# Attention with its sums of squares in the outputs' PSUM bank, later rotation ends, moved ramp buffers and fewer small softmax operations

## Chip, cores, metric

The kernel runs on one core of a Trainium2 chip. The core has five engines, each with a queue of its own that it works off in order: TensorE (PE, matrix products; its weight loads are listed as PEld), VectorE (DVE), ScalarE (ACT), GpSimd (POOL) and SyncE (SP, which here only issues DMAs; POOL issues some as well). The metric is device time in microseconds; a kernel's time is the median of its runs.

## The reference, cut to what matters

Two layers over 528 tokens (16 learned meta tokens and 512 others) of width 2048. Layer 0 mixes tokens by softmax attention, layer 1 by gated linear attention. Around each: `h <- h + post_norm(mixer(pre_norm(h)))`. The change is mostly in layer 0:

```
def attention_mixer(h, w_in, q_norm, k_norm, w_out, ang_row, ang_col):
    q, k, v, gate = split(h @ w_in)          # 16 q heads, 8 k and v heads, of 128; gate of 2048
    q = apply_axial_rope(rmsnorm(q, q_norm), ang_row, ang_col)      # norm per head, then rotation
    k = apply_axial_rope(rmsnorm(k, k_norm), ang_row, ang_col)
    s = einsum(q, k) * 128 ** -0.5           # each k, v head serves two q heads
    p = softmax(s)
    o = einsum(p, v)
    return (o * silu(gate)) @ w_out
```

Layer 1 projects q, k, v, an output gate and two low-rank decay gates (one per direction), sums the log gates along the tokens, and computes decayed scores and outputs per head (4 heads). Its output, normed and gated, goes through `w_out`, is normed, added to `h`, and the 512 real tokens are stored.

## The kernel before, in words

**Precision.** Products of float32 are made of three products: each operand is split into a rounded part and a remainder (`split`: a cast on ScalarE, line 135, and a subtraction on VectorE, line 136), and high x high, high x low and low x high are summed in PSUM (lines 158 to 160 for the projections). So each weight block of 512 KB costs a DMA (`wraw`), a cast (`whi`) and a subtraction (`wlo`), and 48 matmuls for each half of the tokens (264 columns).

**Order of the work.** Instructions are written in the order of a clock kept in Python (`Clock`): each three projection matmuls of 264 columns step it by 0.339 us, so a projection of 128 columns of weights over both halves steps it by 10.84. Side work hangs on it: generators that `yield` a delay (`drive`), and functions put off by `after`. That gives a program order; the compiler's planner then places each instruction on its engine's queue by that priority, by when its buffers and inputs are free in its model, and it adds the semaphore waits. On the chip, the order of each queue is fixed.

**Stages.** (1) *Start*: `x` is loaded, transposed, and the first three gate columns projected. (2) *Ramp of layer 0*: K0, Q0, Q1, V0 are projected and stored in DRAM (`qkv_d`), then gates 3 to 12 by a seven-product scheme (`seven`; its combined inputs are `th`, `tl`, in the profile `t0h`, `t0l`; `quarters` are raw weight blocks, `y` the results on their way to `g_d`). (3) *Attention*: eight groups `g` of one k, v head and two q heads. While the scores and outputs of group g are computed (`attention`), the projections of group g + 1 are written between them (`qkv`: K, Q, Q, V; for g + 1 = 1 V comes first). Group 0 has no projection there; its tiles come back from DRAM (`first_group`, `one_head`). (4) *Output projection and residual*, the low-rank gates, a ramp of layer 1 that is like the first. (5) *Gated linear attention*, four heads. (6) *Last projection*, four token tiles in turn, each finished and stored by `finish_token`.

**What the change touches in stage 3.** `take` makes `qw` (the head times its norm weight) and `sq` (its squares) while evacuating the projection's PSUM banks (tag `pp`, three of them), lines 291 and 292. `rope` swaps the quarters of `qw` by four DMAs into `qs` (SP), splits `sq` into `sh`, `sl`, multiplies by cosine and sine on POOL (lines 304, 305), and puts off its end, `late`, by 3.7 of the clock: per half of the tokens two matmuls with ones (`ssq`, lines 310 and 311) that sum the squares over partitions, an evacuation on VectorE into `f`, which is the `sq` tile (line 312), then a reciprocal root on ScalarE, the two halves of the rotation added (line 314), times `f` (line 315), and split into `qh`, `ql` or `kh`, `kl`. `softmax` computes a block of scores `s` (128 queries x 528 keys, one pair of banks), its maximum (627), the maximum times -SCALE (628), the exponential with its sum (631), the reciprocal (632), and the scaling of `pn`: 512 columns (633), and the last 16 three times over, for an 80-row transposed operand (635). `transposed` transposes `pn` into `pT` and `pTm` (lines 641, 643; both with tag `t`, two banks in turn) and splits them into `ph`, `pl`, `pmt`. `weighted` accumulates the outputs in the one bank with tag `o` (lines 661 to 664), copied out by ScalarE (665). `values` transposes V by way of the `t` banks too (`vps`, `vpm`, lines 551 to 563). `stored_gates` loads gates, applies SiLU (line 610 on POOL) and stores gated outputs. Of PSUM's eight banks three are `pp`, two `s`, two `t`, one `o`. A block of scores takes one slot of the clock (`SLOTS[g]`), and there are nine blocks and a last step for each group.

**In stages 4 and 5.** `token_major` copies rows of `h` through `hb` to DRAM. `gates(h)` loads the low-rank weights of head h, splits them into `ups`, and makes log gates: `z` (matmul `pz`, line 1044; ScalarE, line 1045), `e`, and running sums. `load_v` brings V back through `vt`, one tile of 512 columns at a time, and splits it.

Of the kernel before, what the change touches and what calls it, by code (L numbers as in the profile page):

```python
# [10 lines left out]
F32 = mybir.dt.float32  # L11
# [8 lines left out]
P = 128  # L20
D = 2048
# [13 lines left out]
AHEAD = 400  # L35
SLOTS = (2.6, 3.8, 3.8, 3.8, 3.8, 3.8, 3.8, 2.6)

# [45 lines left out]
def hybrid_encoder(  # L83
# [201 lines left out]
    def take(wcol):  # L285

        qw = wk.tile([P, T], F32, tag="qw", name="qw")
        sq = wk.tile([P, T], F32, tag="sq", name="sq", bufs=1)

        def evac(ps, a, b):  # L290
            A.activation(qw[:, a:b], ps, AF.Copy, scale=wcol)
            A.activation(sq[:, a:b], ps, AF.Square)
        return qw, sq, evac

    def rope(qw, sq, outs, ps_t):
        qs = wk.tile([P, T], F32, tag="qs", name="qs", bufs=1)
# [10 lines left out]
        def late():  # L307
            for a, b in HALVES:
                ps = ps_t.tile([P, 512], F32, tag="t", name="ssq")[:, :b - a]
                PE.matmul(ps, ones_r, sh[:, a:b], start=True, stop=False)  # L310
                PE.matmul(ps, ones_r, sl[:, a:b], start=False, stop=True)
                V.scalar_tensor_tensor(f[:, a:b], ps, 1.0 / P, erow[:, a:b], op0=ALU.mult, op1=ALU.add)
            rsqrt_inplace(f)
            V.tensor_tensor(qw, qw, qs, op=ALU.add)
            V.tensor_tensor(qw, qw, f, op=ALU.mult)
            for hi, lo, a, b in outs:
                split(hi, lo, qw[:, a:b])
        clk.after(3.7, late)

# [168 lines left out]

    la = ExitStack()
    yp = pool(la, "yp0", 2)  # L490
    ta = pool(la, "ta0")
    quarters = [ta.tile([P, 4 * HALF], F32, name=f"x0{i}") for i in range(4)]
    th, tl = [ta.tile([P, KH, 4 * HALF], F32R, name=f"t0{w}") for w in "hl"]

# [34 lines left out]
    REP = 80  # L529
    pn_bufs = [pb.tile([P, T + REP], F32, name=f"pn{i}") for i in range(NP)]  # L530
    for t in pn_bufs:
# [6 lines left out]
    def values(g):  # L538
# [4 lines left out]
        if g == 0:  # L543
            nc.gpsimd.dma_start(out=vt, in_=qkv_d[3])
        else:
# [30 lines left out]
    def first_group(outs):  # L576

        qws = []
        for i in range(4):
            if i < 3:  # L580
                qws.append(wk.tile([P, T], F32, tag="qw", name="qw"))
                nc.gpsimd.dma_start(out=qws[i], in_=qkv_d[i])
            if i:
                one_head(qws[i - 1], outs[i - 1], i - 1)
            yield 3.8

    def one_head(qw, outs, i):
        sq = wk.tile([P, T], F32, tag="sq", name="sq", bufs=1)
        A.activation(sq, qw, AF.Square)
        A.activation(qw, qw, AF.Copy, scale=col(QN if i else KN))  # L590
        rope(qw, sq, outs, ps_t)

# [26 lines left out]
    def softmax(n, qh, ql, kh, kl):  # L619
# [6 lines left out]
        sm = wa.tile([P, 1], F32, tag="sm", name="sm")[:n]  # L626
        V.reduce_max(mx, s, axis=AX.XY)  # L627
        V.tensor_scalar(mx, mx, -SCALE, None, op0=ALU.mult)  # L628
        pn = pn_bufs[n_pn[0] % NP][:n]
        n_pn[0] += 1  # L630
        A.activation(pn[:, :T].rearrange("p (a b) -> p a b", a=2), s, AF.Exp, bias=mx, scale=SCALE, accum_out=sm)  # L631
        V.reciprocal(sm, sm)
        V.tensor_scalar(pn[:, :SEQ], pn[:, :SEQ], sm, None, op0=ALU.mult)
        for r in (0, 32, 64):
            V.tensor_scalar(pn[:, T + r:T + r + META], pn[:, SEQ:T], sm, None, op0=ALU.mult)
        return pn

    def transposed(pn, n, puts):
# [3 lines left out]
        pm = ps_t.tile([P, 512], F32, tag="t", name="pTm")[:REP]  # L642
        PE.transpose(pm[:, :n], pn[:, T:], ident[:n, :n])
        for (ph, pl, pmt), qc, c, m in puts:
# [59 lines left out]
    for g in range(KV):  # L704
        o_sb = o_tiles()
        att = attention(qk, vv, o_sb, SLOTS[g])
        att = clk.drive(att if g else chain(first_group(first_outs), att))
        gates = [] if g == 0 else [2 * g - 2, 2 * g - 1]
# [10 lines left out]
        if g + 1 < KV:  # L719
# [130 lines left out]
    def token_major(k, t):  # L850
# [7 lines left out]
        A.activation(hb, ps, AF.Square, accum_out=s1[:n, t, k // 4:k // 4 + 1])  # L858
# [98 lines left out]
    quarters += [ta.tile([P, 4 * HALF], F32, name=f"x{i}") for i in range(2, 4)]  # L957

    def token_rows(ys, vc):

        c = slice(vc * P, (vc + 2) * P)
        for ts in ((0, 1), (2, 3), (4,)):
# [6 lines left out]
            for n, t in enumerate(ts):  # L969
# [55 lines left out]


    def gates(h):
        ur = g2.tile([P, SEQ], F32, tag="gr", name="ur", bufs=1)[:16].rearrange("p (d n) -> p d n", d=2)
        nc.sync.dma_start(out=ur, in_=gla_gk_up[0, :, :, h * 256:(h + 1) * 256].rearrange("d r n -> r d n"))
        yield 4.0  # L1030
        A.copy(ups[0:16], ur)
        A.copy(ups[64:80], ur)
        V.tensor_tensor(ups[32:48], ur, ups[0:16].bitcast(F32), op=ALU.subtract)
# [327 lines left out]
    def finish_token(t, ps):  # L1361
# [3 lines left out]
        A.activation(r, r, AF.Exp, scale=-0.5)  # L1365
        for n in range(2):
            ns = slice(n * 1024, (n + 1) * 1024)
            V.scalar_tensor_tensor(y[t][:, ns], y[t][:, ns], r, h1[t][:, ns], op0=ALU.mult, op1=ALU.add)
# [52 lines left out]
```

## Time and profile before

| | |
|---|---|
| median of 3 runs | 1814.77 us (1813.13 to 1814.82) |
| the profiled execution | 1812.24 us, of which the span of the profile is 1810.5 us |
| mean granted clock of TensorE | 0.995 |

The profile is of one execution. Busy shares are of the span. A row of the stages has from and to, the length, the busy time and count of each engine, the granted TensorE clock (1.00 is full), the busy share of the DMA engines, and GB/s. A row of waits has the waiting engine with the tile that it writes and its line, what it waited for, and the sum, the number and the longest of the waits. A row of instructions has the start, the duration, engine, line, operation, output <- inputs, and in brackets the idle time before it with what ended it. A row of one line's instructions has the shortest, the median and the longest duration in ns, and when the first and the last started. A DMA row of the page has its count, the size of one and the median time from issue to landing.

### The profile page before, as it was taken

How to read it: one execution, taken by the hardware profiler on the slowest of the kernel's cores; microseconds unless marked ns; L12 is line 12 of the kernel's file. 1: busy time of each engine (PE TensorE's matmuls, PEld its weight loads, DVE VectorE, ACT ScalarE, POOL GpSimd, SP SyncE). 2: the span in 40 equal slices, each digit the busy share in tenths (PEclk: the TensorE clock that was granted, in tenths of full speed). 3: DMA queues.
4: the chain of work that ended last, by engine and by line, in shares of the span. 5: the costliest groups of instructions: out<-in, count | busy, mean ns of one | idle time of the engine just before them, and what ended most of it. 6: DMA issues, size and time to landing. Idle time of an engine off the chain costs nothing. (4 is left out here: it accounts for less than half of the span.)

```text
span 1810.5 us, 31970 instructions
## 1 busy us (share of the span) xinstructions
PE 1764.6 (97%) x12591; PEld 1656.8 (92%) x12591; DVE 1147.3 (63%) x2118; ACT 951.1 (53%) x1909; POOL 218.1 (12%) x291
## 2 busy tenths in 40 slices
PE   8999889999999999999999999999999999999998
PEld 7999888999999999999999999988898988888886
DVE  5777578766766766752229787758585765764224
ACT  5543456555555555553328544468575775853221
POOL 3100222112121111111111101110000100000000
PEclk9999989999999999999999999999999999999999
DMA  8444422323233233153336344343332332354323
GB/s 255 143 140 119 153 75 86 89 83 95 71 95 95 60 95 112 66 174 86 91 96 201 118 140 118 106 136 89 86 108 71 108 101 80 100 157 169 98 93 128
DMA packets 266453, 203.12 MB, mean 112 GB/s; under 512 B 9884, under 2 KB 239840, under 8 KB 265776
## 3 DMA queue, kind: packets, MB, share of 16 engines
q1 hardware_dynamic: 254480, 162.52, 31.3%
q0 software_dynamic: 11824, 38.57, 6.1%
q8 instruction: 99, 1.62, 0.4%
q14 instruction: 50, 0.41, 0.1%
HBM read 165.47 MB, written 29.09 MB: 107 GB/s over the span
## 5 line engine op out<-in xcount | busy, mean ns | idle before, releaser
L158 PE MATMUL pp<-uh,whi 128*128 128x264 f32 (+1 forms) x2320 | 711.8, 307 | 1.2 <-POOL whi L357 0.6
L159 PE MATMUL pp<-ul,whi 128*128 128x264 f32 (+1 forms) x2320 | 702.7, 303 | 2.3 <-DVE ul L419 2.3
L160 PE MATMUL pp<-uh,wlo 128*128 128x264 f32 (+1 forms) x2320 | 703.3, 303 | 0.3 <-POOL wlo L358 0.3
L136 DVE TENSOR_TENSOR wlo<-wraw,whi 128x1024 fp32r<-128x1024 f32 (+1 forms) x239 | 293.5, 1229 | 289.1 <-ACT whi L135 288.3
L160 PEld LDWEIGHTS pp<-uh,wlo 128*128 128x128 f32 x2320 | 437.5, 189 | 17.5 <-POOL wlo L358 0.6
L158 PEld LDWEIGHTS pp<-uh,whi 128*128 128x128 f32 x2320 | 437.6, 189 | 17.2 <-POOL whi L357 0.9
L159 PEld LDWEIGHTS pp<-ul,whi 128*128 128x128 f32 x2320 | 438.0, 189 | 16.2 <-DVE ul L419 2.7
L135 ACT CAST whi<-wraw 128x1024 fp32r<-128x1024 f32 (+1 forms) x239 | 249.1, 1043 | 291.5 <-PE pp L159 95.2
L135 ACT CAST whi<-x 128x1024 fp32r<-128x1024 f32 x48 | 50.1, 1047 | 71.4 <-PE pp L236 55.5
L631 ACT ACTIVATE pn<-s,mx 128x528 f32<-128x528 f32 (+1 forms) x72 | 50.4, 700 | 67.0 <-DVE mx L628 61.8
L1333 PE MATMUL f<-whi,ul 128*128 128x512 f32 x192 | 75.6, 394 | 0.0
L1331 PE MATMUL f<-whi,uh 128*128 128x512 f32 x192 | 75.5, 393 | 0.0
L1332 PE MATMUL f<-wlo,uh 128*128 128x512 f32 x192 | 75.3, 392 | 0.0
L237 PE MATMUL pp<-uh,wlo 128*128 128x264 f32 x264 | 75.2, 285 | 0.0
L235 PE MATMUL pp<-uh,whi 128*128 128x264 f32 x264 | 75.0, 284 | 0.0
L236 PE MATMUL pp<-ul,whi 128*128 128x264 f32 x264 | 74.7, 283 | 0.0
L136 DVE TENSOR_TENSOR wlo<-x,whi 128x1024 fp32r<-128x1024 f32 x48 | 58.6, 1222 | 20.0 <-ACT whi L135 19.9
L304 POOL TENSOR_TENSOR qw<-qw,cos 128x528 f32<-128x528 f32 x24 | 32.2, 1340 | 287.4 <-DMA qs<-qw 261.0
L646 DVE TENSOR_TENSOR pl<-pT,ph 128x512 fp32r<-128x512 f32 (+1 forms) x80 | 47.3, 592 | 17.1 <-ACT ph L645 16.7
L627 DVE TENSOR_REDUCE mx<-s 128x1 f32<-128x528 f32 (+1 forms) x72 | 50.7, 704 | 8.9 <-PE s L624 7.6
L645 ACT CAST ph<-pT 128x512 fp32r<-128x512 f32 (+1 forms) x80 | 40.4, 505 | 30.0 <-PE pT L641 24.2
L235 PE MATMUL pp<-th,whi 128*128 128x264 f32 x192 | 55.8, 292 | 0.0
(401 smaller groups left out, 3734.5 us busy)
## 6 DMA issues: line engine op xcount, KB each, us to landing
wraw<-in_attn_w_in_dram SPq DMA_DIRECT2D x82, 512.0 KB, 4.2
wraw<-in_gla_w_in_dram SPq DMA_DIRECT2D x81, 512.0 KB, 3.9
wraw<-in_attn_w_out_dram SPq DMA_DIRECT2D x32, 512.0 KB, 3.9
wraw<-in_gla_w_out_dram SPq DMA_DIRECT2D x32, 512.0 KB, 3.8
x<-in_gla_w_in_dram SPq DMA_DIRECT2D x15, 512.0 KB, 4.4
qs<-qw SPq DMA_DIRECT2D x96, 66.0 KB, 3.1
x<-in_attn_w_in_dram SPq DMA_DIRECT2D x12, 512.0 KB, 4.3
x<-h_d SPq DMA_DIRECT2D x32, 132.0 KB, 3.2
```

The source lines that it names most:

```text
L135: A.copy(hi, src)
L136: V.tensor_tensor(lo, src, hi.bitcast(F32), op=ALU.subtract)
L158: PE.matmul(ps, wh, uh[:, k, a:b], start=first, stop=False)
L159: PE.matmul(ps, wh, ul[:, k, a:b], start=False, stop=False)
L160: PE.matmul(ps, wl, uh[:, k, a:b], start=False, stop=last)
L235: PE.matmul(ps, w[0][:, k], bh[:, k], start=k == 0, stop=False)
L236: PE.matmul(ps, w[0][:, k], bl[:, k], start=False, stop=False)
L237: PE.matmul(ps, w[1][:, k], bh[:, k], start=False, stop=k == KH - 1)
L627: V.reduce_max(mx, s, axis=AX.XY)
L1331: PE.matmul(ps, uh[:, k, ts], wh[:, kk], start=(k == 0), stop=False)
L1332: PE.matmul(ps, uh[:, k, ts], wl[:, kk], start=False, stop=False)
L1333: PE.matmul(ps, ul[:, k, ts], wh[:, kk], start=False, stop=(k == KT - 1))
```

## The change

- `rope`: the `ssq` matmuls of both halves go to the outputs' bank (tag `o`) instead of the `t` banks; the end comes 6.5 of the clock later (4.5 for group 0's heads) instead of 3.7. `qw` has three buffers instead of two, `sq` two instead of one.
- The norm weight of q is multiplied by SCALE once; the maximum is negated by the reduction itself; the multiplication by -SCALE goes. The three copies of the last 16 columns become one operation with a broadcast input.
- Ramp of layer 0: `th`, `tl` are placed first in memory, `y` and the quarters behind them.
- Group 0: all three loads of `qw` are issued at the start; V's load goes to SP's queue; the heads follow at 1.0, 4.6, 4.6 and 5.0 instead of 3.8 each. Group 0's slot is 3.1 instead of 2.6; group 1's scores start 7.0 later.
- Layer 1: the low-rank weights of head 0 are loaded and split (`up_rows`) ahead of the ramp's projections; the forward `z` tiles of head 0 lie in `vt`'s buffer; `load_v(0)` has no delay of 16 any more; `hb` has four buffers instead of five.
- `finish_token`: the last token tile is finished in pieces of 1024, 640 and 384 columns instead of 1024 and 1024.

```diff
-SLOTS = (2.6, 3.8, 3.8, 3.8, 3.8, 3.8, 3.8, 2.6)
+SLOTS = (3.1, 3.8, 3.8, 3.8, 3.8, 3.8, 3.8, 2.6)
...
-        qw = wk.tile([P, T], F32, tag="qw", name="qw")
-        sq = wk.tile([P, T], F32, tag="sq", name="sq", bufs=1)
+        qw = wk.tile([P, T], F32, tag="qw", name="qw", bufs=3)
+        sq = wk.tile([P, T], F32, tag="sq", name="sq", bufs=2)
...
-    def rope(qw, sq, outs, ps_t):
+    def rope(qw, sq, outs, ps_t, wait=6.5):
...
-                ps = ps_t.tile([P, 512], F32, tag="t", name="ssq")[:, :b - a]
+                ps = ps_o.tile([P, 512], F32, tag="o", name="ssq")[:, :b - a]
...
-        clk.after(3.7, late)
+        clk.after(wait, late)
...
+    V.tensor_scalar(col(QN), col(QN), SCALE, None, op0=ALU.mult)
...
+    ta = pool(la, "ta0")
+    th, tl = [ta.tile([P, KH, 4 * HALF], F32R, name=f"t0{w}") for w in "hl"]
     yp = pool(la, "yp0", 2)
-    ta = pool(la, "ta0")
     quarters = [ta.tile([P, 4 * HALF], F32, name=f"x0{i}") for i in range(4)]
-    th, tl = [ta.tile([P, KH, 4 * HALF], F32R, name=f"t0{w}") for w in "hl"]
...
-            nc.gpsimd.dma_start(out=vt, in_=qkv_d[3])
+            nc.sync.dma_start(out=vt, in_=qkv_d[3])
...
-        for i in range(4):
-            if i < 3:
-                qws.append(wk.tile([P, T], F32, tag="qw", name="qw"))
-                nc.gpsimd.dma_start(out=qws[i], in_=qkv_d[i])
-            if i:
-                one_head(qws[i - 1], outs[i - 1], i - 1)
-            yield 3.8
+        for i in range(3):
+            qws.append(wk.tile([P, T], F32, tag="qw", name="qw", bufs=3))
+            nc.gpsimd.dma_start(out=qws[i], in_=qkv_d[i])
+        for i in range(3):
+            yield 4.6 if i else 1.0
+            one_head(qws[i], outs[i], i)
+        yield 5.0
...
-        V.reduce_max(mx, s, axis=AX.XY)
-        V.tensor_scalar(mx, mx, -SCALE, None, op0=ALU.mult)
+        V.reduce_max(mx, s, axis=AX.XY, negate=True)
...
-        for r in (0, 32, 64):
-            V.tensor_scalar(pn[:, T + r:T + r + META], pn[:, SEQ:T], sm, None, op0=ALU.mult)
+        V.tensor_scalar(pn[:, T:].rearrange("p (r m) -> p r m", r=3)[:, :, :META],
+                        pn[:, SEQ:T].unsqueeze(1).broadcast_to([n, 3, META]), sm, None, op0=ALU.mult)
...
-        att = clk.drive(att if g else chain(first_group(first_outs), att))
+        lead = first_group(first_outs) if g == 0 else iter([7.0] if g == 1 else [])
+        att = clk.drive(chain(lead, att))
...
+    ups = c1.tile([80, 2, 256], F32R, name="ups")
+    G.memset(ups.bitcast(F32), 0.0)
...
-        hb = t2.tile([P, 512], F32, tag="hb", name="hb", bufs=5)[:n]
+        hb = t2.tile([P, 512], F32, tag="hb", name="hb", bufs=4)[:n]
...
+    def up_rows(h, ur):
+        ur = ur.rearrange("p (d n) -> p d n", d=2)
+        nc.sync.dma_start(out=ur, in_=gla_gk_up[0, :, :, h * 256:(h + 1) * 256].rearrange("d r n -> r d n"))
+        yield 4.0
+        A.copy(ups[0:16], ur)
+        A.copy(ups[64:80], ur)
+        V.tensor_tensor(ups[32:48], ur, ups[0:16].bitcast(F32), op=ALU.subtract)
...
     built = clk.drive(combine(th, tl, quarters))
+    clk.drive(up_rows(0, sa.tile([16, SEQ], F32, name="ur", bufs=1)))
...
     def gates(h):
-        ur = g2.tile([P, SEQ], F32, tag="gr", name="ur", bufs=1)[:16].rearrange("p (d n) -> p d n", d=2)
...
+        if h:
+            yield from up_rows(h, g2.tile([P, SEQ], F32, tag="gr", name="ur", bufs=1)[:16])
...
-                z = g2.tile([P, T], F32, tag="z", name="z", bufs=1)[:, :n]
+                z = g2.tile([P, T], F32, tag="vt" if h == d == 0 else "z", name="z", bufs=1)[:, :n]
...
-        if h in (0, 3):
-            yield 24.0 if h else 16.0
+        if h == 3:
+            yield 24.0
...
-        for n in range(2):
-            ns = slice(n * 1024, (n + 1) * 1024)
+        for a, b in ((0, 1024), (1024, D)) if t < 3 else ((0, 1024), (1024, 1664), (1664, D)):
+            ns = slice(a, b)
```

More of the change, by code (lines that the diff above doesn't have):

```diff
@@ L529, in hybrid_encoder @@
     REP = 80
-    pn_bufs = [pb.tile([P, T + REP], F32, name=f"pn{i}") for i in range(NP)]
+    pn_bufs = [pb.tile([P, T + 96], F32, name=f"pn{i}") for i in range(NP)]
     for t in pn_bufs:
@@ L578, in first_group @@
         qws = []
-        for i in range(4):
-            if i < 3:
-                qws.append(wk.tile([P, T], F32, tag="qw", name="qw"))
-                nc.gpsimd.dma_start(out=qws[i], in_=qkv_d[i])
-            if i:
-                one_head(qws[i - 1], outs[i - 1], i - 1)
-            yield 3.8
+        for i in range(3):
[5 more added lines that the diff above has]
+        yield 5.0
     def one_head(qw, outs, i):
-        sq = wk.tile([P, T], F32, tag="sq", name="sq", bufs=1)
+        sq = wk.tile([P, T], F32, tag="sq", name="sq", bufs=2)
         A.activation(sq, qw, AF.Square)
         A.activation(qw, qw, AF.Copy, scale=col(QN if i else KN))
-        rope(qw, sq, outs, ps_t)
+        rope(qw, sq, outs, ps_t, 4.5)
     def stored_gates(hs, held):
@@ L626, in softmax @@
         sm = wa.tile([P, 1], F32, tag="sm", name="sm")[:n]
-        V.reduce_max(mx, s, axis=AX.XY)
-        V.tensor_scalar(mx, mx, -SCALE, None, op0=ALU.mult)
+        V.reduce_max(mx, s, axis=AX.XY, negate=True)
         pn = pn_bufs[n_pn[0] % NP][:n]
         n_pn[0] += 1
-        A.activation(pn[:, :T].rearrange("p (a b) -> p a b", a=2), s, AF.Exp, bias=mx, scale=SCALE, accum_out=sm)
+        A.activation(pn[:, :T].rearrange("p (a b) -> p a b", a=2), s, AF.Exp, bias=mx, accum_out=sm)
         V.reciprocal(sm, sm)
         V.tensor_scalar(pn[:, :SEQ], pn[:, :SEQ], sm, None, op0=ALU.mult)
-        for r in (0, 32, 64):
-            V.tensor_scalar(pn[:, T + r:T + r + META], pn[:, SEQ:T], sm, None, op0=ALU.mult)
+        V.tensor_scalar(pn[:, T:].rearrange("p (r m) -> p r m", r=3)[:, :, :META],
+                        pn[:, SEQ:T].unsqueeze(1).broadcast_to([n, 3, META]), sm, None, op0=ALU.mult)
         return pn
@@ L642, in transposed @@
         pm = ps_t.tile([P, 512], F32, tag="t", name="pTm")[:REP]
-        PE.transpose(pm[:, :n], pn[:, T:], ident[:n, :n])
+        PE.transpose(pm[:, :n], pn[:, T:T + REP], ident[:n, :n])
         for (ph, pl, pmt), qc, c, m in puts:
@@ L727, in hybrid_encoder @@
     slots = [wk.tile([P, T], F32, tag=tag, name="ogr", **kw) for tag, kw in
-             (("qw", {}), ("qw", {}), ("qs", dict(bufs=1)), ("sq", dict(bufs=1)))]
+             (("qw", dict(bufs=3)), ("qw", dict(bufs=3)), ("qs", dict(bufs=1)), ("sq", dict(bufs=2)))]
     slots.append(wa.tile([P, T], F32, tag="vt", name="ogr", bufs=1))
@@ L1005, in hybrid_encoder @@
     vm = cg.tile([80, 512], F32R, name="vm")
-    ups = cg.tile([80, 2, 256], F32R, name="ups")
     kfs = [cg.tile([P, 2, T], F32, name=f"kf{i}") for i in range(2)]
@@ L1011, in hybrid_encoder @@
     nc.sync.dma_start(out=qf[:, 0], in_=kq_d[2][:, :SEQ])
-    for t in am + [vm, ups]:
+    for t in am + [vm]:
         G.memset(t.bitcast(F32), 0.0)
@@ L1027, in gates @@
     def gates(h):
-        ur = g2.tile([P, SEQ], F32, tag="gr", name="ur", bufs=1)[:16].rearrange("p (d n) -> p d n", d=2)
[L1029 to L1033, printed above, removed]
+        if h:
+            yield from up_rows(h, g2.tile([P, SEQ], F32, tag="gr", name="ur", bufs=1)[:16])
         yield 2.0
```

## The prediction

> **What bounds the kernel now.** I read the busy times first, then the span cut into stages, then TensorE's waits.
>
> ```profile
> PE 1764.6 (97%) x12591; PEld 1656.8 (92%) x12591; DVE 1147.3 (63%) x2118; ACT 951.1 (53%) x1909; POOL 218.1 (12%) x291
> ```
>
> TensorE (PE) is busy 97% of the span, and the change alters the count or shape of no large matmul. What can be won is idle time of PE, and time at a lower clock. The stages (first column: from and to, in us; then length and busy time of each engine):
>
> ```profile
> 205.00:340.00 135.00, 120.36 (x926) 115.84 (x925) 95.53 (x218) 76.30 (x167) 31.75 (x34) 0.95 0.36 104
> 340.00:580.00 240.00, 230.76 (x1869) 225.66 (x1868) 168.35 (x401) 135.30 (x303) 45.82 (x43) 1.00 0.30 86
> 580.00:760.00 180.00, 177.88 (x1446) 174.22 (x1446) 130.03 (x330) 97.02 (x227) 22.76 (x21) 1.00 0.29 85
> 1180.00:1210.00 30.00, 27.36 (x176) 23.95 (x175) 13.53 (x19) 15.35 (x25) 6.83 (x15) 1.00 0.56 165
> 1210.00:1802.80 592.80, 592.22 (x3263) 511.37 (x3261) 353.75 (x620) 341.51 (x719) 23.40 (x43) 1.00 0.35 105
> 1802.80:1810.50 7.70, 0.00 (x0) 0.00 (x0) 3.23 (x4) 1.17 (x4) 0.00 (x0) 0.69 0.61 242
> ```
>
> Softmax attention (205 to 760) has 14.6 + 9.2 + 2.1 = 25.9 us of idle PE, the start of the gated layer 2.6, its remaining 593 us only 0.6, the tail 7.7. The waits of PE say who ends that idle time (total, times, longest):
>
> ```profile
> PE ssq L310 <- DVE pl L646: 8.6, 13, 1.3
> PE ssq L310 <- DVE vm L562: 6.8, 1, 6.8
> PE pT L641 <- DVE pn L633: 3.7, 2, 3.5
> PE s L622 <- ACT pn L631: 2.6, 2, 1.3
> PE pTm L643 <- DVE vl L555: 1.6, 3, 0.5
> PE pz L1044 <- ACT z L1045: 1.6, 1, 1.6
> PE s L622 <- ACT qh L135: 0.8, 1, 0.8
> PE pz L1044 <- DVE ups L1033: 0.7, 1, 0.7
> ```
>
> Two long stalls also cost clock. The stretches right behind them:
>
> ```profile
> 225.60:228.80 3.20, 3.15 (x14) 3.15 (x15) 2.44 (x4) 0.37 (x2) 1.75 (x2) 0.50 0.17 42
> 256.10:263.00 6.90, 6.49 (x27) 5.73 (x28) 5.21 (x11) 3.13 (x10) 3.05 (x2) 0.51 0.16 39
> ```
>
> The column before the last two is the granted clock. Behind the 6.8 us stall PE worked 3.15 us at half speed, which loses 1.6; behind the 3.5 us stall 6.49 us, which loses 3.2. The stalls of 1.3 us left no such stretch. So the ceiling is 25.9 + 2.6 + 1.6 + 3.2 = 33 us, 1.8%, unless the tail shrinks.
>
> In a sentence apart: the Trainium skill, TensorE: Matmul & The Clock Gate, Part 1, gives half clock after about 3.4 us idle and full clock after about 3.4 us of sustained work; by the latter the second stall would lose 1.7 instead of 3.2, and my sum would be 19.8 instead of 21.3. The trace shows 6.9 us, and the measurement decides.
>
> **The change part by part.**
>
> *Loads of group 0 (all three q/k tiles asked for at once, `vt` moved from POOL's queue to SP's, the ramp's `th`/`tl` placed where the attention's tiles come to lie, `y` and the quarters above).*
>
> ```profile
> 216.88 1.33 POOL L610 TENSOR_TENSOR gs<-gs,gr 128x528 f32<-128x528 f32 x1 [6.95 <-ACT gs L145]
> 218.18 1.11 POOL L582 DMA_DIRECT2D qw<-qkv_d  x2
> ACT sq L589 <- DMA qw<-qkv_d: 2.4, 1, 2.4
> 205.00:210.00 5.00, 5.00 (x43) 5.00 (x42) 2.09 (x3) 1.05 (x1) 2.60 (x7) 1.00 1.03 330
> L237 PE MATMUL pp<-t0h,wlo x160: 280/283/289, 109.4 to 202.5; 128*128 128x264 f32 x160
> ```
>
> The first head's loads leave POOL at 218.18, behind a multiplication that waited 6.95 us; ScalarE then stands 2.4 us on the landing, with the evacuations of `vps` queued behind it, `vm` comes last of these, and PE's `ssq` waits for the bank that `vm` reads: 6.8 + 1.6 = 8.4 us. In the new layout the tiles lie over `th`/`tl` (`t0h`, `t0l` in the profile), last read at 202.5 by the row above, not over the `y` tiles that are still being stored; the loads can leave some 10 us earlier, and `ssq` no longer shares a bank with `vps`. `vt` on SP is one issue among the weight loads, and one less on POOL. Late next is the rest of the head's chain, under 1.4 us of PE by my guess from the 1.3 us stalls above. I take 7.0 (bounds 0 and 8.4).
>
> *`sq` twice, `qw` three times, rotation's end at 6.5 instead of 3.7.*
>
> ```profile
> 247.23 0.84 ACT L291 ACTIVATE qw<-pp,cols 128x264 f32<-128x264 f32 x2
> 258.36 0.67 ACT L292 ACTIVATE sq<-pp 128x264 f32<-128x264 f32 x2
> DVE qw L314 <- POOL qs L305: 15.6, 13, 3.0
> ```
>
> Group 1's first head is copied out of PSUM at 247.23, but its squares only at 258.36, 11 us later: the single `sq` is still the factor of group 0's last head. So the projection banks stay full, PE has no projection to put between, and stands 3.5 us at `pT`. VectorE in turn stands 15.6 us in all at `L314` for POOL's rotation, with softmax work queued behind it; ending the rotation 2.8 later lets that work go first. With two `sq` the bank is freed at once. I take 6.0 of 3.5 + 3.2 (bounds 0 and 6.7), and 1.0 of the `s` waits of 2.6 + 0.8 (0 and 3.4). `ssq` later delays `kh`, `qh`; the 10.8 clock-us V projection of the code covers that, and group 1, whose V comes first, gets a lead of 7.0 before its scores.
>
> *Sums of squares in the outputs' bank.*
>
> ```profile
> 225.65 0.59 PE L310 MATMUL ssq<-sh,ones_r 128*128 128x264 f32 x1 [6.78 <-DVE vm L562]
> 229.23 0.28 PE L310 MATMUL ssq<-sh,ones_r 128*128 128x264 f32 x1
> L311 PE MATMUL ssq<-sl,ones_r x48: 280/284/422, 226.0 to 709.6; 128*128 128x264 f32 x48
> L312 DVE SCALAR_TENSOR_TENSOR sq<-ssq,erow x48: 419/423/435, 227.6 to 713.4; 128x264 f32<-128x264 f32 x48
> L315 DVE TENSOR_TENSOR qw<-qw,sq x24: 684/707/710, 232.5 to 715.3; 128x528 f32<-128x528 f32 x24
> ```
>
> `ssq` leaves the two banks of `pT`, so the 8.6 us on `pl` go. But the outputs have one bank: in each of the 24 rotations (48 halves) the second half's matmuls must wait until `L312` has read the first, at least 0.284 + 0.423 = 0.71 us, and an output that follows waits for the second read. The program order is laid out with other matmuls in such gaps: the halves at 225.65 and 229.23 lie 3.6 us apart with projections between. So the price is between 0 and 24 x 0.71 = 17.0. Nearest is what a half waited for so far, 8.6 / 48 = 0.18 each, since it is again VectorE running behind the order: 24 x 0.18 = 4.3. Net gain 4.3 (bounds 8.6 and -8.4).
>
> *Fewer small softmax operations.*
>
> ```profile
> L628 DVE TENSOR_SCALAR mx<-mx x72: 131/153/155, 249.4 to 754.6; 128x1 f32<-128x1 f32 x64, 32x1 f32<-32x1 f32 x8
> L635 DVE TENSOR_SCALAR pn<-pn,sm x216: 216/227/1349, 251.5 to 756.8; 128x16 f32<-128x16 f32 x96, 32x16 f32<-32x16 f32 x12
> ```
>
> 72 `L628` at 0.153 go: 11.0 us of VectorE. 216 `L635` become 72 of 48 elements; at 0.227 each (a little above, at most the 0.7 of the 528-element rows) some 33 us of VectorE go in all when summed by duration. The added scaling of one column is one operation like `L628`, beside PE's ramp. VectorE is not the bound (394 of 555 us busy in these stages), so PE gets only what waited on its tail: I take 1.0 (0 and the 1.6 of `pTm`).
>
> *Slots.* Group 0 takes 15.2 lead (as before: 4 x 3.8 = 1.0 + 4.6 + 4.6 + 5.0) plus ten slots: 41.2 clock-us before, 46.2 after; group 1 38 before, 45 after. Their cover is four projections, 43.4. The overrun of 2.8 + 1.6 = 4.4 is covered by the next group's projections, which need none of it: 0 (bounds 0 and a loss of 4.4).
>
> *Start of the gated layer.*
>
> ```profile
> L1031 ACT CAST ups<-ur x4: 602/619/620, 1194.9 to 1502.7; 16x512 fp32r<-16x512 f32 x4
> 1201.11 0.62 ACT L135 CAST vh<-vt 128x512 fp32r<-128x512 f32 x1 [0.74 <-DMA vt<-v_d]
> ```
>
> The first `ups` (one SP load, two casts of 0.62, a subtraction, a POOL memset) moves ahead of the ramp's projections, which cover it: the 0.7 goes. `z` takes `vt`'s buffer, so the V loads come behind the gates, and ScalarE no longer stands on a landing in the middle of their chain: most of the 1.6 goes. I take 2.0 (0 and 2.3). `load_v` without its delay of 16 starts later in effect, under projections.
>
> *`hb` 5 to 4.*
>
> ```profile
> h_d<-hb POOLq DMA_DIRECT2D x16, 256.0 KB, 3.6
> L858 ACT ACTIVATE hb<-ht x20: 571/588/623, 959.9 to 1008.8; 128x512 f32<-128x512 f32 x16, 16x512 f32<-16x512 f32 x4
> ```
>
> 20 in 49 us is one per 2.4; four buffers last 9.8, a store lands in 3.6: 0.
>
> *Last token tile in three pieces.*
>
> ```profile
> 1805.50:1806.50 1.00, 0.00 (x0) 0.00 (x0) 1.00 (x2) 0.00 (x0) 0.00 (x0) 0.64 0.14 53
> 1806.50:1809.00 2.50, 0.00 (x0) 0.00 (x0) 0.24 (x1) 0.00 (x0) 0.00 (x0) 0.50 1.00 398
> L1368 DVE SCALAR_TENSOR_TENSOR y<-y,rt,h x8: 1277/1282/1285, 1791.7 to 1805.5; 128x1024 f32<-128x1024 f32 x8
> ```
>
> A smaller last piece looks like a shorter tail, but from 1806.5 to 1809.0 the DMA engines are full at 398 GB/s: 1 MB, both pieces of 512 KB back to back, and its start hangs on the first piece, which is unchanged. The last pieces arrive in time to queue behind it: 0 (0.3 either way).
>
> **Sum**: 7.0 + 6.0 + 1.0 + 4.3 + 1.0 + 2.0 = 21.3. The profiled execution took 1812.24, so 1790.9 by it; it lies 2.5 below the median of 1814.77, against which I forecast 1793.5.
>
> **The rivals.**
>
> 1. *The second half waits uncovered* (chance 0.10). The order puts nothing between the halves; each rotation pays the full 0.71: 17.0 in place of 4.3, a gain of 8.6, 1806.2. For it: one bank; against it: the 3.6 us with projections between the halves above. Apart from the sum: the Trainium skill, PSUM — Partial Sum Buffer, Summary: rules for kernel authors, says to aim at a different bank when PSUM is read while matmuls run, which speaks against this change; by that rule the price would be the 17.0. No run here yet shows one bank for both.
>
> 2. *Slower: the shared bank behind weight splits* (0.07). The row that decides:
>
> ```profile
> L136 DVE TENSOR_TENSOR wlo<-wraw,whi x239: 678/1225/1905, 5.7 to 1787.2; 128x1024 fp32r<-128x1024 f32 x118, 128x512 fp32r<-128x512 f32 x2
> ```
>
> If such a split stands ahead of `L312` on VectorE in half of the rotations, they pay 24 x 0.71 + 12 x 1.225 = 31.7. The other gains are 17.0, and the 8.6 still go: 31.7 - 25.6 = 6.1 slower, 1820.9. It decides from 25.6 / 24 = 1.07 us a rotation. Against it: a half so far waited 0.18 on the same engine.
>
> 3. *Group 0's stalls only move* (0.11). Three loads of 264 KB fall together with weights at a DMA share of 1.03; at 330 GB/s they hold these up by 2.4 us, and any stall like those of 3.5 brings its slow stretch with it. Without the 7.0 and the 6.0 the gain is 8.3: 1806.5. For it: 6.8 us of PE ended on one late landing already; against it: PE is busy 5.00 of 5.00 us in that very stretch.
>
> 4. *The cover of groups 0 and 1 fails* (0.10): the overrun of 4.4 is paid, gain 16.9, 1797.9.
>
> 5. *The change does not do what it says* (0.05): each wait that goes is replaced by the next engine's at the same place, and the time stays within 3.6 us of before.
>
> **How the numbers follow.** The forecast has the rest, 0.57. It and rivals 1, 3 and 4 are faster: 0.88; rival 5 the same, 0.05; rival 2 slower, 0.07. (0.2% is 3.6 us, about what a measurement of this kernel can tell from no change.) With every upper bound the gain is 8.4 + 6.7 + 3.4 + 8.6 + 1.6 + 2.3 + 0.3 = 31.3: 1783.5, the lower end, rounded down. The upper end, 1807, takes in rivals 1, 3 and 4 and leaves out 2 and 5; the forecast alone would lie between 1786 and 1801.
>
> **What would show it.** Right: idle PE of the stage from 205 to 340 falls from 14.6 to under 4, with no stretch at clock 0.5 in it; the pairs of `L291` and `L292` lie within 2 us of each other; no `ssq` waits on `pl` or `vm`; `ssq` waits on `L312` add up to about 4; `pz` waits under 0.5; the last DMA stretch still runs 2.5 us at about 398 GB/s. The forecast is wrong if `ssq` waits on `L312` by more than 0.7 each (rivals 1 and 2), if a stall of over 3 us stands anywhere in group 0 (rival 3), or if `s` or `pT` waits grow where groups 0 and 1 end (rival 4).

## The result: 0.9% slower

| | before | after |
|---|---|---|
| median, runs of one comparison | 1813.95 us (1812.07 to 1814.82) | 1830.48 us (1827.41 to 1833.35) |
| ratio, 95% interval | | 1.0092 (1.0073 to 1.0111) |
| the profiled execution, its span | 1812.24, 1810.5 us | 1830.27, 1828.5 us |

The forecast was 1793.5 us with a range of 1783 to 1807. The change is some 16.5 us slower, and the span grew by 18.0. First the page of after, then the first and last score matmul of each kernel (line 622 before, 623 after; the two times are the starts, in us).

```profile
PE 1769.3 (97%) x12591; PEld 1662.5 (91%) x12591; DVE 1121.6 (61%) x1904; ACT 950.8 (52%) x1909; POOL 219.7 (12%) x290
```

```profile
L622 PE MATMUL s<-kh,qh x144: 280/284/589, 245.5 to 753.2; 128*128 128x264 f32 x128, 128*32 128x264 f32 x16
```

```profile
L623 PE MATMUL s<-kh,qh x144: 278/284/422, 242.8 to 767.8; 128*128 128x264 f32 x128, 128*32 128x264 f32 x16
```

The scores took 507.7 us and now take 525.0: 17.3 of the 18.0 us lie inside the attention. The same stages as before, of after:

```profile
205.00:340.00 135.00, 121.68 (x950) 117.73 (x949) 91.16 (x172) 76.74 (x166) 34.92 (x35) 0.96 0.37 107
340.00:580.00 240.00, 223.43 (x1772) 219.36 (x1771) 150.67 (x302) 129.97 (x293) 39.76 (x37) 0.97 0.28 81
580.00:760.00 180.00, 173.34 (x1401) 170.18 (x1400) 113.83 (x233) 95.62 (x220) 25.09 (x22) 0.99 0.29 86
```

Idle TensorE: 13.3 us in the first stage (14.6 before), 16.6 in the second (9.2), 6.7 in the third (2.1). The granted clock, 1.00 in the last two stages before, is 0.97 and 0.99: TensorE lost time and speed. VectorE has less to do, as intended (150.67 against 168.35 us in the middle stage). What TensorE waited for, of after:

```profile
PE ssq L310 <- DVE sq L312: 20.5, 12, 3.4
PE vps L552 <- DMA vt<-qkv_d: 4.5, 1, 4.5
PE ssq L311 <- DVE sl L136: 3.4, 2, 3.1
...
PE pz L1051 <- ACT z L1052: 0.7, 1, 0.7
```

`ssq` no longer waits for `pl` (8.6) or `vm` (6.8). In their place the second half's matmuls wait 20.5 us for VectorE's `L312` to read the first half out of the one bank. The prediction had 4.3 for this. What VectorE itself waited for at the addition, before in the prediction (15.6 in 13), of after:

```profile
DVE qw L314 <- POOL qs L305: 40.1, 19, 3.5
```

The later end was to shorten this wait; it went from 15.6 to 40.1 us. One rotation in the timeline of after (start, duration; idle before and its cause in brackets) shows how the two belong together:

```profile
353.45 1.32 POOL L304 TENSOR_TENSOR qw<-qw,cos 128x528 f32<-128x528 f32 x1 [18.10 <-DMA qs<-qw]
...
354.44 0.29 PE L310 MATMUL ssq<-sh,ones_r 128*128 128x264 f32 x1
...
354.73 1.31 POOL L305 TENSOR_TENSOR qs<-qs,sin 128x528 f32<-128x528 f32 x1
...
356.08 0.71 DVE L314 TENSOR_TENSOR qw<-qw,qs 128x528 f32<-128x528 f32 x1 [2.56 <-POOL qs L305]
...
356.89 0.49 DVE L633 TENSOR_SCALAR pn<-pn,sm 128x512 f32<-128x512 f32 x1
357.30 0.24 DVE L634 TENSOR_SCALAR pn<-pn,sm 128x48 f32<-128x48 f32 x1
357.46 0.42 DVE L312 SCALAR_TENSOR_TENSOR sq<-ssq,erow 128x264 f32<-128x264 f32 x1
...
357.93 0.39 PE L310 MATMUL ssq<-sh,ones_r 128*128 128x264 f32 x1 [1.92 <-DVE sq L312]
```

The first half is summed at about 354.9. `L312`, which frees the bank, runs at 357.46: ahead of it on VectorE's queue stand the addition `L314`, which idles 2.56 us for POOL, and the softmax tail (the reciprocal, `L633` and `L634`). In the order of after's queue the addition stands ahead of the first `L312` in 20 of 24 rotations; before, in 3. A likely reason, read from these orders and waits alone: with the sums due later, the planner found the addition ready first and placed it first, but on the chip POOL came later than in the plan. In another rotation a third late item stands there, the gate's product, which waits for its load:

```profile
505.34 0.29 PE L310 MATMUL ssq<-sh,ones_r 128*128 128x264 f32 x1
...
507.01 0.71 DVE L601 TENSOR_TENSOR gr<-gr,rrow 128x528 f32<-128x528 f32 x1 [3.23 <-DMA gr<-g_d]
...
508.90 0.71 DVE L314 TENSOR_TENSOR qw<-qw,qs 128x528 f32<-128x528 f32 x1 [1.19 <-POOL qs L305]
509.64 0.43 DVE L312 SCALAR_TENSOR_TENSOR sq<-ssq,erow 128x264 f32<-128x264 f32 x1
510.13 0.39 PE L310 MATMUL ssq<-sh,ones_r 128*128 128x264 f32 x1 [3.39 <-DVE sq L312]
```

Of the twelve waits for `L312`, nine have an addition that waits for POOL between the first sum and its read: 16.2 of the 20.5 us, this last rotation among them. One more, 2.4 us, has the gate's product alone, and two, 2.0 us together, have the softmax tail and the split of `pT`.

These stalls cost a second time. The stretch in which the stall of 1.92 us lies, and the two behind it, cut where the granted clock changes:

```profile
354.87:358.29 3.42, 1.50 (x13) 1.29 (x13) 2.18 (x6) 0.74 (x2) 1.18 (x1) 1.00 0.00 0
358.29:361.70 3.41, 3.41 (x18) 3.41 (x17) 1.73 (x4) 1.87 (x3) 0.00 (x0) 0.50 0.00 0
361.70:365.11 3.41, 3.41 (x30) 3.41 (x29) 2.50 (x5) 2.01 (x5) 0.59 (x1) 1.00 0.50 141
```

Behind it TensorE issued 18 matmuls in 3.41 us at half clock instead of 30. In the attention there are eight such stretches of 3.41 us in after, four before (two times 6.8 us). Four of the eight follow directly on a stall for `L312`; at 1.7 us of lost work each, these cost 6.8 us. Between the first and the last score there are five stretches in after and two before. Three more make 5.1 us, and with the waits (20.5 in place of 8.6: 11.9) that is 17.0 us, about the growth of 17.3 that the scores show.

### The profile page after: what moved, and what is told of

Read it like the earlier page. It is cut to its first block, busy times and chain, and to the rows that moved or that the text cites. A ratio compares the mean times of both kernels' runs of the same rounds, so it can differ in the third digit from the quotient of the medians.

```text
span 1828.5 us, 31687 instructions
## 1 busy us (share of the span) xinstructions
PE 1769.3 (97%) x12591; PEld 1662.5 (91%) x12591; DVE 1121.6 (61%) x1904; ACT 950.8 (52%) x1909; POOL 219.7 (12%) x290
## 5 line engine op out<-in xcount | busy, mean ns | idle before, releaser
L136 DVE TENSOR_TENSOR wlo<-x,whi 128x1024 fp32r<-128x1024 f32 x48 | 58.6, 1222 | 20.5 <-ACT whi L135 20.5
L646 DVE TENSOR_TENSOR pl<-pT,ph 128x512 fp32r<-128x512 f32 (+1 forms) x80 | 47.4, 593 | 21.4 <-ACT ph L645 20.7
```

The lines of the kernel that those rows point to most:

```text
L136: V.tensor_tensor(lo, src, hi.bitcast(F32), op=ALU.subtract)
```

## The experiments

The theory that came out of the traces (A below): what decides is what stands ahead of the first `L312` on VectorE's queue, and whether that waits. Its rivals: one bank costs by itself, a later end costs by itself, or POOL's lateness alone counts. All ratios are to the kernel before, run beside the experiment. The names "end 3.7" and "end 6.5" are the delay of a rotation's end; group 0 keeps 4.5 wherever the changed kernel is the base. The planner orders the whole program anew after each edit, so an experiment changes one thing in the source, but the order of the queues can differ in other places as well. One table sets the two places of the sums against each other in five surrounds:

| surround | sums in the two `t` banks | sums in the outputs' bank |
|---|---|---|
| all else changed, end 6.5 | 0.9984 (0.9974 to 0.9994) | 1.0092 (1.0073 to 1.0111) |
| all else changed, end 3.7 | 0.9944 (0.9929 to 0.9960) | 0.9942 (0.9923 to 0.9961) |
| the same, `vt` on POOL's queue | 0.9923 (0.9906 to 0.9939) | 0.9917 (0.9902 to 0.9932) |
| before, end 3.7 | 1 | 1.0010 (1.0000 to 1.0019) |
| before with the small softmax operations | 0.9975 (0.9965 to 0.9984) | 1.0011 (1.0002 to 1.0020) |

In none of the five is the one bank faster beyond the intervals.

**Undoing the bank, the end, or both.**

```diff
 # e1: the changed kernel, bank undone
-                ps = ps_o.tile([P, 512], F32, tag="o", name="ssq")[:, :b - a]
+                ps = ps_t.tile([P, 512], F32, tag="t", name="ssq")[:, :b - a]
 # e2: the changed kernel, end undone
-    def rope(qw, sq, outs, ps_t, wait=6.5):
+    def rope(qw, sq, outs, ps_t, wait=3.7):
 # e3: both
```

> The changed kernel with the ssq matmuls back in the two banks of pT, end of the rotation still at 6.5. Theory 1 (order and bank together: at 6.5 the addition of L314, which waits for POOL, stands ahead of L312 in VectorE's queue, and with one bank PE waits for L312 between the halves): the waits of ssq on L312 (20.5 us) and their slow clock (4 stretches, 6.8 us) go, some waits on pl come back (up to 8.6), so about 1806 (1800 to 1814). Theory 2 (one bank is enough by itself): 1800 to 1810 as well. Theory 3 (the later end by itself, k and q arriving late): unchanged, 1825 to 1833.

> The changed kernel with the rotation's end at 3.7 (4.5 stays for group 0), ssq still in the outputs' bank; L314 then stands behind the first L312 in VectorE's queue in every rotation. Theory 1: ssq waits on L312 fall from 20.5 to under 7 us, no stall over 2 us at ssq, time about 1804 (1798 to 1811). Theory 2: waits on L312 stay above 15 us, 1823 to 1833. Theory 3: ssq waits shrink little, but the time falls below 1810 because k and q come earlier.

> Both undone: ssq in the banks of pT, end at 3.7; what is left is the rest of the change. All theories: faster than before by the rest's own worth. From the profile of the changed kernel against before (startup of group 0 about 4 us better, gated layer 2 us, fewer small operations 1 to 4 us): 1802 to 1811; waits of ssq on pl of 5 to 11 us are back.

Measured: e1 1810.97 us, e2 1803.11, e3 1804.75. The waits on the sums, of e1, of e2, of e3:

```profile
PE pT L641 <- DVE sq L312: 8.5, 6, 1.7
```

```profile
PE ssq L310 <- DVE sq L312: 1.4, 3, 0.7
```

```profile
PE ssq L310 <- DVE pl L646: 6.7, 6, 2.2
```

Neither part alone does the whole harm, as theory 1 had it. With end 3.7 one bank costs 1.4 us of waits, and time equals that of two banks. With two banks the later end costs 0.40% (7 us): `pT` waits 8.5 us for a bank that `L312` has not read, in place of 6.7 us for `pl`, and waits for the copy of `vt` and for the exponential (3.0 and 2.6 us) come to it. Together they cost 1.5% against e2. Whatever holds `L312` back passes on: with two banks to the transposes, with one to the second half at once.

**Taking the addition off VectorE.**

```diff
 # e4: the changed kernel
         G.tensor_tensor(qs, qs, sin, op=ALU.mult)
+        G.tensor_tensor(qw, qw, qs, op=ALU.add)
...
-            V.tensor_tensor(qw, qw, qs, op=ALU.add)
```

> The changed kernel (shared bank, end at 6.5) with the addition of L314 done by POOL right behind its two multiplications, so that nothing that waits for POOL stands ahead of L312 on VectorE; 24 more POOL operations of 1.3 us. Theory 1: ssq waits on L312 under 5 us, 1796 to 1808. Theory 2: waits stay above 15 us, 1823 to 1833. Theory 3: 1823 to 1833, since k and q come no earlier.

Measured: 1819.43 us, 1.0033 (1.0022 to 1.0045), 11 us better than after. The wait of e4 (`L313` is the read here, `L311` the sum):

```profile
PE ssq L311 <- DVE sq L313: 16.2, 11, 2.7
```

This lies between the theories (1796 to 1808, or 1823 and above), so the addition is one cause and not the only one. But the edit isn't clean: of the 16.2 us, 4.5 stand behind the gate's product in two rotations, 1.5 in group 0, and 10.2 in eight rotations behind a softmax tail that had become longer. In seven of these eight the 48-column scaling `L634` runs beside an operation of POOL, in five the moved addition (`L306` here), and takes some 1.3 us; in the rotation of after above it took 0.24. In all, ten of the 72 scalings are so slow in e4, two in after. One of them, of e4:

```profile
412.05 1.36 POOL L306 TENSOR_TENSOR qw<-qw,qs 128x528 f32<-128x528 f32 x1
...
412.18 1.28 DVE L634 TENSOR_SCALAR pn<-pn,sm 128x48 f32<-128x48 f32 x1
```

So the addition on POOL took away one late item and slowed another.

**Other ends: 7.5 and 5.0.**

> The changed kernel with the rotation's end at 7.5 instead of 6.5. Theory A (place in the queue): one bank costs only what stands ahead of the first L312 on VectorE; 7.5 is 3.7 plus one softmax slot of 3.8, so L312 falls at the same point of the softmax cycle as with 3.7, and POOL has had 1.0 us more than with 6.5: TensorE waits for L312 under 8 us in all, 1803 to 1812. Rival B (a later end is itself what costs, as the addition still stands ahead of the first half in 20 of 24 rotations): 20 us of these waits or more, 1828 or above. Rival C (only POOL's lateness counts): twelve rotations, each 1.0 us better, so some 9 us of waits are left, 1815 to 1820.

> The changed kernel with the rotation's end at 5.0, halfway. The addition L314 then stands ahead of the first half in 10 of 24 rotations (0 with 3.7, 20 with 6.5). Theory A: waits and time between the two, about 10 us of waits for L312, 1813 to 1820. Rival B (the cost grows with the delay alone): 1803.1 + (1830.5 - 1803.1) x 1.3 / 2.8 = 1816, the same; the two differ in the place of the waits: by A they stand in the ten rotations with the addition ahead, by B in all.

Measured: 7.5 gave 1812.77 us, 0.9991 (0.9978 to 1.0003); 5.0 gave 1818.26, 1.0017 (1.0007 to 1.0027). Waits for `L312` in e5, then in e6:

```profile
PE ssq L310 <- DVE sq L312: 13.7, 11, 2.4
```

```profile
PE ssq L310 <- DVE sq L312: 14.6, 9, 3.9
```

The cost does not grow with the delay: 3.7, 5.0, 6.5 and 7.5 give 1803, 1818, 1830 and 1813. That rules out a price of lateness as such (B). A was too good for 7.5, and C alone doesn't do either: in e5 the addition is done in time in many rotations, and this one waits for nothing:

```profile
459.58 0.71 DVE L314 TENSOR_TENSOR qw<-qw,qs 128x528 f32<-128x528 f32 x1 [2.28 <-POOL qs L305]
...
464.34 0.43 DVE L312 SCALAR_TENSOR_TENSOR sq<-ssq,erow 128x264 f32<-128x264 f32 x1 [0.20 <-PE ssq L311]
```

while in others the addition, the softmax tail and the split of `pT` (`L646`) still stand between the first half and its read. For 5.0 both A and B had expected its time. Of its nine stalls six lie in rotations with the addition ahead, as A said; four of them (8.7 of the 14.6 us) have it between the first sum and its read. The other three, 5.4 us, stand behind the split of `pT`, which waits for ScalarE.

**The bank alone, in the kernel before.**

> The kernel before with one thing changed: the sums of squares in the outputs' bank (end at 3.7 as before). Theory A: the first L312 has no late item ahead of it, so the second half waits little, and the 8.6 us of waits for pl go: 1805 to 1811. Rival (the second half always pays its 0.71 us): 17 less 8.6, 1822 or more.

Measured: 1816.14 us, 1.0010, no gain. The wait of e7:

```profile
PE ssq L310 <- DVE sq L312: 9.8, 12, 3.3
```

Both ideas missed: not 17 us, but also no gain of 4 to 9. The 8.6 us for `pl` became 9.8 for `L312`. No item that waits stands there: in eleven of the twelve rotations VectorE works through the softmax tail or the split of `pT` first, and in the twelfth, the 3.3 us, one scaling of 16 columns took 3.02 us while POOL ran the rotation's multiplications.

**The small softmax operations alone, and with the bank.**

> The kernel before with only the smaller softmax tail (reduce_max that negates, one broadcast operation for three, the scale in the q norm column); sums of squares in the two banks of pT, end at 3.7. The prediction's term: 1.0 us, so 1814, the same. Rival: VectorE's room ahead of pl and pT is worth more, since 13 waits for pl of 8.6 us in all depend on when VectorE comes to it: 1808 or below, waits for pl under 4.

> The same with the sums of squares in the outputs' bank as well, end at 3.7. Theory D: the shorter softmax work on VectorE is what makes one bank cheap with this end (waits for L312: 9.8 us in 12 with the long softmax work, 1.4 in 3 in the changed kernel with end 3.7): under 4 us of waits for L312, 5 us or more below the run with the small operations alone or with the bank alone. Rival E: the other parts (buffers of sq, loads) make it cheap: waits for L312 stay at 8 to 10 us, and the time equals the small operations alone.

Measured: e9 1809.20 us (0.9975), e10 1815.72 (1.0011). The small operations are worth some 4.5 us, between the 1.0 of the prediction and the 6 or more of the rival. In e10 the wait for `L312` fell from 9.8 to 2.1 as theory D said, but the time is 6.5 us above e9, against it. Where it went, in the waits of e10:

```profile
PE vps L552 <- ACT vt L547: 8.1, 4, 3.1
...
PE ssq L310 <- DVE sq L312: 2.1, 3, 1.5
```

and one of these four, in its timeline:

```profile
438.15 0.71 DVE L601 TENSOR_TENSOR gr<-gr,rrow 128x528 f32<-128x528 f32 x1 [4.42 <-DMA gr<-g_d]
...
445.73 0.69 PE L552 MATMUL vps<-ident,vt 128*128 128x128 f32 x2 [3.12 <-ACT vt L547]
```

The move gave the planner another order; now the gate's product waits 4.42 us for its load, the head behind it is late, and ScalarE's copy of `vt` behind that. The chain between these two rows is read from the trace and was not tried by itself. Most of the 6.5 us is slow clock: the attention of e10 has seven half-clock stretches of 3.41 us, that of e9 four, and three make 5.1 us.

**The read on ScalarE: is it VectorE's queue?**

```diff
 # e13: the changed kernel, end 6.5, one bank; e16: the same with end 3.7 and vt on POOL
-                V.scalar_tensor_tensor(f[:, a:b], ps, 1.0 / P, erow[:, a:b], op0=ALU.mult, op1=ALU.add)
+                A.activation(f[:, a:b], ps, AF.Copy, scale=1.0 / P)
+            V.tensor_tensor(f, f, erow, op=ALU.add)
```

> The changed kernel (one bank, end 6.5) with the bank of the sums read by ScalarE (a scaled copy) instead of VectorE's L312; the addition of erow is one more VectorE operation of 528 columns, behind both reads. Theory A (VectorE's queue is the cause): waits of the second half under 8 us, 1806 to 1815, although VectorE has 24 x 0.3 us more work. Rival F (one bank with this end costs whoever reads it): waits of 15 us or more, now for ScalarE, 1823 or above.

> One bank, end 3.7, vt on POOL, the sums read by ScalarE. Theory A: L312's waits are only 2.1 us there, so little is to be won, 1798 to 1801. Rival: ScalarE stands behind its exponentials and silu steps more often than VectorE, 1803 or above.

Measured: e13 1806.78 us, 0.9957 (0.9942 to 0.9972): 24 us below the changed kernel, with the same bank and the same end. VectorE has a little less work (24 additions of 0.71 us, 17.0, in place of 48 reads of 0.42, 20.2), not more as was expected; 3 us less work cannot give 24. Its wait for the read, and a rotation (`L312` is ScalarE's read, `L315` the addition):

```profile
PE ssq L310 <- ACT sq L312: 1.3, 4, 0.8
```

```profile
481.53 1.31 POOL L305 TENSOR_TENSOR qs<-qs,sin 128x528 f32<-128x528 f32 x1
...
482.01 0.39 ACT L312 ACTIVATE sq<-ssq 128x264 f32<-128x264 f32 x1 [0.33 <-PE ssq L311]
...
482.88 0.71 DVE L315 TENSOR_TENSOR qw<-qw,qs 128x528 f32<-128x528 f32 x1 [2.30 <-POOL qs L305]
```

The addition still waits 2.30 us for POOL, and no longer matters: the bank was read at 482.01. With the same bank and the same end the waits are gone. So the 20.5 us were not the price of one bank, nor of a late end, but of what stands ahead of the read on its engine. e16 gave 1805.21, 0.9948 (0.9934 to 0.9963), slower than e8 below: its rival was right. Where nothing late stands ahead on VectorE, ScalarE is the worse reader (6.5 us of waits for its `L312`).

**The gate's product on POOL as well.**

```diff
 # e14: e4, and
-            V.tensor_tensor(gr, gr, rrow, op=ALU.mult)
+            G.tensor_tensor(gr, gr, rrow, op=ALU.mult)
```

> The changed kernel with the addition L314 and the stored gates' product L601 (it waits for its load) on POOL. In the run with the addition alone on POOL 16.2 us of waits for L312 were left in 11 rotations, some 3 us each in those that the trace puts down to the gate's product. If that reading is right, 6 to 10 us of them go: 1809 to 1814. If all of it is the softmax tail: 16 us stay, 1819.

Measured: 1812.28 us, 0.9985 (0.9976 to 0.9994), 7 us below e4 and in the range expected, but the waits for the read fell by 3.4 us, not by 6 to 10:

```profile
PE ssq L311 <- DVE sq L313: 12.8, 8, 4.0
```

The two waits behind the product (4.5 us in e4) are gone, so it was a cause too. Of the 12.8 us, 4.0 (1.5 in e4) stand in group 0, behind a multiplication that waits for POOL's addition; the other 8.8 stand behind the softmax tail, in six of its seven rotations again with a slow `L634` beside POOL. Neither was tried alone.

**Group 0, and the best version.**

> The changed kernel with the end at 3.7, and the load of vt back on POOL's queue. If the stall of 4.8 us at the first vps is due to the place of this load behind a waiting one on SP's queue, it goes, with the half-clock stretch of 6.8 us behind it (3.4 us of work lost): 1795 to 1799. If the stall only moves to another landing of group 0, the time stays at 1803 and a stall of 3 us or more stands elsewhere between 210 and 260.

> The best version so far with the sums back in the two banks of pT: end 3.7, vt on POOL. If one bank is worth the prediction's 4.3: 1804. If it is worth nothing once nothing late stands ahead of the read: 1799 to 1801, with waits for pl of 5 to 8 us in place of those for L312.

> The kernel of end 3.7 and vt on POOL's queue, with sq in one buffer as before. The prediction's term for the buffers: 6.0 (a stall of 3.5 us at pT and its half-clock stretch, 3.2): 1806, with L291 and L292 of group 1's first head some 10 us apart and a half-clock stretch near 256. Rival: the new spacing of group 0's heads had already cured it, and the second buffer does nothing: 1800, the pair within 2 us.

> The kernel of end 3.7 and vt on POOL's queue, with the addition L314 of group 0's three heads on POOL (the later groups' stays on VectorE). There the addition waited 4.0 us for POOL ahead of the second head's split sl, and TensorE stood 4.1 us at ssq L311 for sl, with 6.8 us of half clock behind it. Theory A: 4 + 3 us less, 1793, no half-clock stretch between 210 and 260. Rival: the stall only moves to the next thing late in group 0 (a landing, or the scores): 1798 to 1801.

e8 (`nc.gpsimd` for the load of `vt` again) gave 1799.85 us, 0.9917 (0.9902 to 0.9932): the stall of 4.8 us at the first `vps` went, and e2's time fell by 3.3. With two banks the same move gains 0.21% (e3 against e15). The intervals overlap in both pairs, so the gain is likely, not shown. A stall of about the same size stands elsewhere, as the rival said:

```profile
223.87 1.79 DVE L314 TENSOR_TENSOR qw<-qw,qs 128x528 f32<-128x528 f32 x1 [4.01 <-POOL qs L305]
...
226.59 0.59 PE L311 MATMUL ssq<-sl,ones_r 128*128 128x264 f32 x1 [4.08 <-DVE sl L136]
```

Again it is the addition, waiting for POOL, ahead of what TensorE needs. e12 moved group 0's additions to POOL; that stall went and another took its place, 1801.44 us, 0.9935 (0.9920 to 0.9950). Its rival was right that the stall moves:

```profile
PE vps L552 <- ACT vt L547: 9.2, 3, 5.7
```

e15, e8 with two banks, gave 1800.85: in the best surround the bank is worth nothing, with 6.8 us of waits for `pl` in place of 2.1 for `L312`. e11, e8 with one `sq`, gave 1803.61, 0.9944 (0.9927 to 0.9960; the intervals of e8 and e11 overlap a little), and the old stall came back with its half-clock stretch of 6.8 us:

```profile
254.09 0.63 PE L641 MATMUL pT<-ident,pn 128*128 128x128 f32 x4 [2.91 <-DVE pn L633]
```

The best kernels are e8 and e15, not to be told apart, 15 us below before and 30 below the change as made.

## Why the prediction was wrong

**The step that failed: "Sums of squares in the outputs' bank".** The mechanism was named (the second half waits until `L312` has read the first, and VectorE runs behind the order), but its price was put at 24 x 0.18 = 4.3. The runs show 20.5 with this end, 9.8 in the kernel before, 1.4 to 2.1 with end 3.7 and the short softmax work. Two things went wrong.

- The 0.18 came from a wait of the old layout, and its cover from one pair of halves 3.6 us apart. That pair was the first, in group 0. In the timeline of before, sixteen of the 24 rotations look like this one, the second half some 0.35 us behind the first:

```profile
360.78 0.39 PE L310 MATMUL ssq<-sh,ones_r 128*128 128x264 f32 x1 [1.27 <-DVE pl L646]
...
361.13 0.36 PE L310 MATMUL ssq<-sh,ones_r 128*128 128x264 f32 x1
```

- The other upper end, 0.71 each, took `L312` to start as soon as its input is there. Rival 2 had the right form, something ahead of `L312` on VectorE, with the deciding price at 1.07 us a rotation. Measured: 20.5 / 24 = 0.85 of waits, and 6.8 / 24 = 0.28 of slow clock, 1.13 together. But it named the weight splits, and in after none of the 24 rotations has one between the first sum and its read. The items that cost most are those that wait themselves: the addition for POOL (16.2 us) and the gate's product for a load. The row for the first, `L314` with 15.6 us, stood in the prediction and was used only for a gain.

Rival 1 named the rule of the Trainium skill, PSUM — Partial Sum Buffer, Summary: rules for kernel authors, to aim at a different bank when PSUM is read while matmuls run. The rule has no price; the 17.0 that the prediction put beside it came from its own rows. It lies near the 20.5 here only by luck: in e2 the same bank cost 1.4, so no run here shows the bank itself as the limit.

**Rotation's end at 6.5.** Booked as part of a gain (1.0 for the `s` waits). With two banks it costs 7 us (e1 against e3), and in after the wait it was to shorten grew from 15.6 to 40.1.

**The slow clock.** "The stalls of 1.3 us left no such stretch" is true, but stalls of 1.8 to 3.4 can, and the sum priced no new one.

**`sq` and `qw` buffers.** Right: e11 brings the stall and the stretch back. The term of 6.0 measures 0.27%, about 5 us, from two comparisons with intervals that overlap a little. The pairs of group 1's first head lie 1.2 us apart, of after:

```profile
241.22 0.48 ACT L291 ACTIVATE qw<-pp,cols 128x264 f32<-128x264 f32 x1 [2.26 <-PE pp L160]
242.38 0.39 ACT L292 ACTIVATE sq<-pp 128x264 f32<-128x264 f32 x1
```

**Small softmax operations.** Undersized: 1.0 against about 4.5 (e9).

**Loads of group 0.** The 7.0 did not come: idle TensorE in the first stage fell from 14.6 to 13.3, not to under 4, and three half-clock stretches of 3.41 us stand in it where the prediction had none. `vm` is no longer late, but `vt` on SP's queue is, which was booked as free; undoing it is worth some 0.25% (e8 against e2; they come from two comparisons, and their intervals overlap). Rival 3 (the stalls only move) holds for group 0, by another cause than the one it gave.

**Start of the gated layer; tail.** The waits of `pz` went from 1.6 + 0.7 to 0.7, near the 2.0 booked; this part was not tried alone. From the start of the last matmul to the last landing it is 7.1 us before and 7.6 after, where 0 (0.3 either way) was said. The last stretch of stores is about as full as before: 2.5 us at 387 GB/s, against 398.

## What to carry to other kernels

When a buffer is made scarcer, don't price it by the two operations that must follow each other; list what stands between them on the reader's queue, and ask of each item what it waits for. Take the pattern from the middle of the loop, not from its first pass. And change a delay in a planned order with the queue in view: 2.8 more moved 20 of 24 additions to the other side of the read, and the ends 3.7, 5.0, 6.5 and 7.5 gave no trend.

## What was not expected of the hardware

**The clock goes by fixed windows, not by the length of a stall.** All half-clock stretches of one run begin and end at multiples of 3.413 us from each other: in after the seven between 218 and 590 lie 0, 6, 41, 64, 86, 91 and 108 windows from the first. Call the stretches of 3.413 us on this grid windows. Over all eighteen kernels, from 60 us to the tail, each of the 43 windows at full clock with 1.9 us or more of idle TensorE was followed by half clock, ten of the 71 with 1.33 to 1.9 us, and none of the others; so about half a window decides. A stall of 2.01 us at 308.17 in after fell across two windows, and nothing followed:

```profile
303.68:307.10 3.42, 2.48 (x21) 2.27 (x19) 2.62 (x5) 1.67 (x3) 0.49 (x1) 1.00 0.32 79
307.10:310.51 3.41, 2.34 (x19) 2.34 (x20) 3.37 (x8) 2.46 (x6) 0.00 (x0) 1.00 0.04 13
310.51:313.92 3.41, 3.41 (x30) 3.41 (x30) 3.25 (x7) 1.99 (x5) 0.00 (x0) 1.00 0.88 247
```

The idle in the first two of these is 0.94 and 1.07 us, against 1.92 in the window shown above. Going back to full clock asks for more: of the 78 windows at half clock, the 25 with 0.38 us or more of idle TensorE were followed by another at half clock, the 53 with 0.32 or less by full clock. The second stall before agrees with this: it cost two windows (3.2 us of work) and not one. The first of the two, of before, holds 0.38 us of idle:

```profile
256.13:259.54 3.41, 3.03 (x11) 2.24 (x12) 2.53 (x8) 2.29 (x7) 0.00 (x0) 0.50 0.33 79
```

The Trainium skill, TensorE: Matmul & The Clock Gate, Part 1, has the free-running window of about 3.4 us, which the trace agrees with, but asks for an idle window; here 1.92 idle of 3.41 was enough. So a stall of 1.8 us, as at 586.75 in after, can cost 1.7 more, by where it falls.

**A small VectorE operation can be slow beside POOL.** In the attention of these kernels the 48-column scaling (`L634` in after) took 0.23 to 0.25 us where POOL ran no operation on tensors for more than half of it (975 times), and mostly 1.3 to 1.65 us where it did (median 1.31 in 49). Reads of PSUM such as `L312` stayed at 0.40 to 0.44 either way. So moving work to POOL has a price on VectorE, as e4 shows.
